# Sixteen experts of a mixture-of-experts stage: order of their matmuls, of the gather and scatter, and of their weight loads

## The chip, the cores and the metric

One core of a Trainium2 chip runs the whole program. The metric is the time of one execution on the device in microseconds, the median of repeated runs.

## The reference

Two transformer blocks run one after the other on 512 tokens of width 1024. Only one stage of the second block is touched, the expert-choice feed-forward: each of 16 experts picks its 64 best tokens, and its answer is added back to them.

```python
def expert_choice_ffn(xn, w_router, w_gate, w_up, w_down):
    cap = CAPACITY_FACTOR * S // N_EXPERTS                     # 64
    aff = softmax(xn @ w_router)                               # 512 x 16
    top_aff, top_idx = lax.top_k(swapaxes(aff, 1, 2), cap)     # per expert
    xg = xn[bidx, top_idx]                                     # gather, 64 x 1024 an expert
    hid = silu(xg @ w_gate) * (xg @ w_up)
    y = (hid @ w_down) * top_aff
    return zeros.at[bidx, top_idx].add(y)                      # scatter
...
h = h + expert_choice_ffn(rmsnorm_2(h, norm_ffn), ...)
ple_gate = sigmoid(rmsnorm_2(h, norm_ple) @ w_ple_gate)
h = h + ple_gate * (p @ w_ple)
return rmsnorm_2(h, norm_final)
```

## The kernel before, in words

Everything ahead of the experts' stage (both mixers, attention, the first block's MLP, the router) is the same in both kernels. A tile framework turns the program text into one instruction list for each engine. Its scheduler goes by program order as a priority and by its own estimate of when data will be there, so a ready instruction can be put ahead of one that the scheduler believes to be waiting; each engine then runs its list strictly in that order.

**Weights.** An expert has three 1024 x 1024 float32 matrices (gate, up, down), loaded as four pieces of 1 MB each: 192 pieces in all. A piece is `wv[:, k:k + 2, :]`, so each of 128 partitions receives two rows of 4 KB that lie 512 KB apart in memory (L806). `load_expert(e + 1)` stands behind expert e in the program; the pieces go into a ring of 15 tiles (`wnext` 12, `wlast` 3), and the first two experts' last pieces into six spare places (`spare`). Twelve pieces are loaded during the output projection ahead of the stage (L1270 to L1275), the others when the stage's pools open. The load instructions are all on SP's queue, in order, and each waits until its ring tile has been read.

**An expert.** 64 tokens make 64 columns of stationary data, so TensorE is used as two halves of 64 columns: the two halves of an output row (512 columns each) go side by side (L1445 for gate and up, L1471 for down). A float32 matmul is two passes in the trace, so gate and up are 64 rows of the trace and down is 32.

1. Gate and up: 64 matmuls into two PSUM banks (`pg`, `pu`).
2. Sigmoid on ScalarE (L1460), two products on VectorE (L1461, L1462).
3. Four transposes on TensorE (L1465), one copy on ScalarE (L1467).
4. Down: 32 matmuls (L1471) that read this copy.
5. `yh`, `yl`: the result times its affinity, split in two parts (ScalarE L1479, VectorE L1480).

**Gather and scatter by pairs.** Experts 2g and 2g+1 share one gather: a one-hot matrix `oh` (VectorE, L1351) picks 128 rows, in eight blocks `rows(k)` of four matmuls (eight rows of the trace, L1360), each block with a ScalarE evacuation into `xg` (L1361). In the text `rows(k + 1)` stands between the gate's matmuls of the even expert; the last pair's gather is taken ahead, behind gate and up of expert 11. Behind the even expert's gate and up come `affinities()` (L1366) and four transposes of `oh` into `gT` (L1457). Behind the odd expert's down come eight scatters: two matmuls (L1483, L1484) and one VectorE addition to `x` (L253) each. The last pair's scatter belongs to the tail, which computes the per-layer gate and the final norm.

**Other work of the stage.** Behind expert 5, `project_p` multiplies `p` by `w_ple` (48 matmuls, L124 to L126). Behind expert 14, `x` is transposed for the tail (L1530). Small pools: `y4` 5 tiles of 4 KB a partition, `m2` 4 tiles of 2 KB. PSUM: `pd` 4 banks, `pscore` 2, `pout` 2.

Software DMAs, issued by GpSimd, occur once, at the start of the second block (13 small loads, L852 to L879).

Of the kernel before, what the change touches and what calls it, by code (L numbers as in the profile page):

```python
# [19 lines left out]
P = 128  # L20
T = 512
# [14 lines left out]
def two_blocks_kernel(ctx: ExitStack, tc: tile.TileContext, A: dict, out: bass.AP, stage: int = 99):  # L36
# [751 lines left out]
    turn = itertools.cycle(["wnext"] * 12 + ["wlast"] * 3)  # L788
# [7 lines left out]
    def load_pieces(e, got):  # L796

        for n in ("w_exp_gate_2", "w_exp_up_2", "w_exp_down_2"):
            wv = A[n][0, e].rearrange("(k p) f -> p k f", p=P)
            for k in range(0, KT, 2):  # L800
                w = spare.pop(0) if e < 2 and len(got) >= 16 + 4 * e else w8()
                if isinstance(w, list):
                    for i in range(2):
                        nc.sync.dma_start(w[i], wv[:, k + i, :])
                else:
                    nc.sync.dma_start(w, wv[:, k:k + 2, :])  # L806
                    w = [w[:, 0, :], w[:, 1, :]]
                got += w
                yield

    spare = []
    started = {}

    def start_expert(e, n):

        if e not in started:
            got = []
            started[e] = got, load_pieces(e, got)  # L820
        for _ in itertools.islice(started[e][1], n):
            pass

    def load_expert(e):
        start_expert(e, 12)
        return started[e][0]


    with ExitStack() as blk:
# [440 lines left out]
        open_ring(late, "wnext", 12, side="right")  # L1270
        start_expert(0, 6)

        def more():
            start_expert(0, 8 - 6)
            start_expert(1, 4)  # L1275
# [32 lines left out]
    with ExitStack() as blk:  # L1308
        pool = blk.enter_context(tc.tile_pool(name="moe", bufs=1, reuse_waits="tile"))
        open_ring(blk, "wlast", 3)  # L1310

        def y4(dt=F32, shape=(D,)):
            return pool.tile([P] + list(shape), dt, name="y4", tag="y4", bufs=5)

        def m2(dt=F32, shape=(T,)):
            return pool.tile([P] + list(shape), dt, name="m2", tag="m2", bufs=4)
# [5 lines left out]
        def pick(ahead=False):  # L1322
            if ahead:
                return m2(shape=(NT, 2, CAP)), y4(shape=(2, KT, CAP))
            return (pool.tile([P, NT, 2, CAP], F32, name="oh", bufs=1),
                    pool.tile([P, 2, KT, CAP], F32, name="xg", bufs=1))

        picked = [pick()]
        w = acts_half(F32, (NT, D), "act_hi")
        spare += [w[:, 0:2, :], w[:, 2:4, :], [y4(), y4()], [y4(), y4()]]  # L1330
# [5 lines left out]
        spare += [w[:, 0:2, :], w[:, 2:4, :]]  # L1336
        ws = load_expert(0)
# [3 lines left out]
        def gather(g):  # L1341

            oh, xg = picked.pop() if picked else pick(ahead=2 * g + 2 == NE)
# [11 lines left out]
            src, sel = (xn[0], oh) if g else (x, scaled)  # L1355

            def rows(k):
                ps = pscore()[:, :P]
                for t in range(NT):
                    PE.matmul(ps, src[:, t, k * P:(k + 1) * P], sel[:, t, :], start=(t == 0), stop=(t == NT - 1))  # L1360
                S.activation(xg[:, :, k, :], ps.rearrange("p (e s) -> p e s", e=2), AF.Copy, scale=gcol[:, k:k + 1])  # L1361
# [9 lines left out]
            return oh, xg, rows, affinities  # L1371

        def load_p():
            pr = w8((NT, 256))
            nc.sync.dma_start(pr, A["p_2"][0, 0].rearrange("(t p) c -> p t c", p=P))
            raw = w8()
            nc.sync.dma_start(raw, A["w_ple_2"][0].rearrange("(k p) c -> p k c", p=P))
            return pr, raw

        def split8(raw):  # L1380
            hi, lo = w8(dt=F32R), w8(dt=F32R)
            S.copy(hi, raw)
            V.tensor_sub(lo, raw, hi.bitcast(F32))
            return hi, lo

        def project_p(pr, raw):
            wh, wl = split8(raw)
            pT = w8((2, 2, T), F32R)
# [41 lines left out]
        oh = xg = None  # L1430
        for e in range(NE):
            if e == NE - 1:
                gfin = row(y4(), A["norm_final_2"])
            if e % 2 == 0 and e + 2 < NE:
                oh, xg, rows, affinities = gather(e // 2)
                rows(0)
            if e == NE - 2:
                oh, xg, _, affinities = ahead
            pg, pu = pd(), pd()
            for i, ps in ((0, pg), (8, pu)):  # L1440
                for k in range(KT):
                    if e % 2 == 0 and e + 2 < NE and i == 0 and k + 1 < KT:
                        rows(k + 1)
                    for half in range(2):
                        PE.matmul(ps[64 * half:64 * half + 64, :], xg[:, e % 2, k, :],  # L1445
                                  ws[i + k][:, 512 * half:512 * half + 512],
                                  start=(k == 0), stop=(k == KT - 1))
            if e == NE - 5:
                ahead = gather(NE // 2 - 1)
                for k in range(KT):  # L1450
                    ahead[2](k)
            if e % 2 == 0:
                affinities()
                yh, yl, gT = y4(F32R), y4(F32R), m2(F32R)
                pt = pout()
                for t in range(NT):
                    PE.transpose(pt[:, t * P:(t + 1) * P], oh[:, t, :], ident)  # L1457
                S.copy(gT, pt)
# [3 lines left out]
            V.tensor_mul(hd, hd, pu)  # L1462
            pt = pout()
            for i in range(4):
                PE.transpose(pt[:, i * P:(i + 1) * P], hd[:, i * P:(i + 1) * P], ident)  # L1465
            hT = m2(shape=(4, P))
            S.copy(hT, pt.rearrange("p (a b) -> p a b", a=4))  # L1467
            py = pscore()
            for k in range(KT):
                for half in range(2):  # L1470
                    PE.matmul(py[64 * half:64 * half + 64, :], hT[:, k % 4, 64 * (k // 4):64 * (k // 4) + 64],  # L1471
                              ws[16 + k][:, 512 * half:512 * half + 512],
                              start=(k == 0), stop=(k == KT - 1))
# [8 lines left out]
            def scatter(t, n, ps):  # L1482
                PE.matmul(ps, gT[:, t * P:(t + 1) * P], yh[:, 512 * n:512 * n + 512], start=True, stop=False)  # L1483
                PE.matmul(ps, gT[:, t * P:(t + 1) * P], yl[:, 512 * n:512 * n + 512], start=False, stop=True)  # L1484
                add_to_x(512 * n)(t, ps)

            last = e == NE - 1 and stage > 7
            if e % 2 and not last:
                for n in range(2):
                    for t in range(NT):  # L1490
                        scatter(t, n, pd())
            if last:
                zh, zl = [[w8((4, T), F32R) for _ in range(2)] for _ in range(2)]
                wg = []
                pss = [pd() for _ in range(NT)]
                todo = [(t, n) for n in range(2) for t in range(NT)]
                for k in range(KT):

                    ps = pout()
                    PE.matmul(ps, yh[:, k * P:(k + 1) * P], gT, start=True, stop=False)  # L1500
                    PE.matmul(ps, yl[:, k * P:(k + 1) * P], gT, start=False, stop=True)
                    zk, hi = xT[k // 4][:, k % 4, :], zh[k // 4][:, k % 4, :]
                    V.tensor_add(zk, zk, ps)
                    S.copy(hi, zk)
                    V.tensor_sub(zl[k // 4][:, k % 4, :], zk, hi.bitcast(F32))
                    if k % 2:
                        wg.append(split_gate(k // 2, wgr[k // 2]))
                        gate_step(pss, k // 2)
                        for _ in range(2):
                            scatter(*todo.pop(0), pscore())  # L1510
            if e == 4:
                praw = load_p()
            if e == 5:
                pp = project_p(*praw)
            if e == 0:
# [4 lines left out]
            if e + 1 < NE:  # L1520
                ws = load_expert(e + 1)
            if e == NE - 2:
                wgr = [load_gate(k) for k in range(0, KT, 2)]

                xT = [w8((4, T)) for _ in range(2)]
                for t in range(NT):
                    for i in range(2):
                        ps = pout().rearrange("p (a b) -> p a b", a=4)
                        for k in range(4):
                            PE.transpose(ps[:, k, :], x[:, t, (4 * i + k) * P:(4 * i + k + 1) * P], ident)  # L1530
                        S.copy(xT[i][:, :, t * P:(t + 1) * P], ps)
# [127 lines left out]
```

## Time and profile before

| | |
|---|---|
| median of 3 runs | 1955.38 us (1954.65 to 1956.43) |
| profiled execution, its own time | 1954.67 us |
| its span, first to last instruction | 1952.9 us |
| TensorE busy | 1878.2 us, 96% of the span |
| VectorE / ScalarE busy | 919.1 us / 718.4 us |
| granted TensorE clock, mean | 0.991 |
| bytes moved | 330.88 MB, 169 GB/s over the span |

The experts' stage runs from about 1383.5 us of the span (first gather) to 1890.9 us (first matmul of the tail). "Busy" of TensorE is modelled at its ends, so the starts of successive matmuls tell more than their durations.

### The profile page before, as it was taken

To read this page: it belongs to the slowest core of one execution; us is meant where nothing else is said; L and a number is where in the kernel's file an instruction comes from. 1 tells how busy PE (TensorE), PEld (TensorE's weight loads), DVE (VectorE), ACT (ScalarE), POOL (GpSimd) and SP (SyncE) were. 2 spreads that over 40 slices of the span, in tenths; PEclk is the share of its full clock that TensorE was granted. 3 is DMA by queue.
4 is the path that set the end of the run, shared out by engine and by line. 5 is a ranking of instruction groups with operands and counts; after the bars stand their busy time and mean duration, and the time that the engine had idled before them with its cause. 6 is when DMAs were issued, how large, how long until landed. Compare 5 with 4: busy or idle time off the path is not lost. (4 is left out here: it accounts for less than half of the span.)

```text
span 1952.9 us, 24468 instructions
## 1 busy us (share of the span) xinstructions
PE 1878.2 (96%) x9723; PEld 1362.9 (70%) x9723; DVE 919.1 (47%) x1659; ACT 718.4 (37%) x1329; POOL 66.9 (3%) x103
## 2 busy tenths in 40 slices
PE   7999999999999999999999999999699999999998
PEld 6777788888888888887787778887344354444346
DVE  5777777465543443436875564453322111111236
ACT  4454774343332322325665554322121121111134
POOL 0000220000000000002000000000000000000000
PEclk9999999999999999999999999999799999999999
DMA  7222226431233333324222222236889999998951
GB/s 206 55 64 72 56 85 189 131 107 55 73 111 98 97 97 97 97 76 112 73 65 57 74 71 70 86 125 247 325 312 402 375 381 401 406 405 334 409 237 44
DMA packets 178052, 330.88 MB, mean 169 GB/s; under 512 B 10766, under 2 KB 90370, under 8 KB 177938
## 3 DMA queue, kind: packets, MB, share of 16 engines
q1 hardware_dynamic: 177522, 328.91, 48.1%
q8 instruction: 77, 1.26, 0.3%
q0 software_dynamic: 416, 0.41, 0.1%
q14 instruction: 37, 0.30, 0.0%
HBM read 327.19 MB, written 2.10 MB: 169 GB/s over the span
## 5 line engine op out<-in xcount | busy, mean ns | idle before, releaser
L104 DVE TENSOR_TENSOR lo<-raw,hi 128x1024 fp32r<-128x1024 f32 x208 | 253.5, 1221 | 324.5 <-ACT hi L103 321.5
L103 ACT CAST hi<-raw 128x1024 fp32r<-128x1024 f32 x208 | 218.0, 1049 | 417.7 <-PE pd L126 230.7
L124 PE MATMUL pd<-hi,act_hi 128*128 128x512 f32 (+2 forms) x584 | 228.2, 391 | 2.0 <-ACT act_hi L206 1.6
L125 PE MATMUL pd<-lo,act_hi 128*128 128x512 f32 (+2 forms) x584 | 226.5, 388 | 0.8 <-DVE lo L104 0.8
L124 PE MATMUL pd<-act_hi,hi 128*128 128x512 f32 (+1 forms) x592 | 224.2, 380 | 0.5 <-ACT act_hi L206 0.5
L126 PE MATMUL pd<-act_hi,lo 128*128 128x512 f32 (+1 forms) x592 | 224.5, 380 | 0.0
L125 PE MATMUL pd<-act_lo,hi 128*128 128x512 f32 (+1 forms) x592 | 224.3, 379 | 0.0
L1445 PE MATMUL pd<-w,xg 128*64 128x512 f32 x896 | 205.3, 598 | 0.0
L126 PE MATMUL pd<-hi,act_lo 128*128 128x512 f32 (+1 forms) x512 | 199.8, 392 | 0.0
L1445 PEld LDWEIGHTS pd<-w,xg 128*64 128x64 f32 x896 | 60.8, 137 | 109.0 <-issue 100.3
L124 PEld LDWEIGHTS pd<-hi,act_hi 128*128 128x128 f32 x584 | 110.3, 189 | 22.7 <-ACT act_hi L206 3.3
L126 PEld LDWEIGHTS pd<-act_hi,lo 128*128 128x128 f32 x592 | 111.5, 188 | 19.5 <-issue 0.2
L125 PEld LDWEIGHTS pd<-act_lo,hi 128*128 128x128 f32 x592 | 111.5, 188 | 19.4 <-DVE act_lo L207 0.5
L124 PEld LDWEIGHTS pd<-act_hi,hi 128*128 128x128 f32 x592 | 111.1, 188 | 19.9 <-ACT act_hi L206 1.0
L125 PEld LDWEIGHTS pd<-lo,act_hi 128*128 128x128 f32 x584 | 110.2, 189 | 20.1 <-DVE lo L104 1.3
L1471 PE MATMUL pscore<-w,m 128*64 128x512 f32 x464 | 107.9, 607 | 6.7 <-ACT m L1467 6.7
L126 PEld LDWEIGHTS pd<-hi,act_lo 128*128 128x128 f32 x512 | 96.7, 189 | 17.9 <-DVE act_lo L207 0.4
L1480 DVE SCALAR_TENSOR_TENSOR y<-pscore,affs,y 64x512 fp32r<-64x512 f32 x32 | 24.0, 750 | 169.2 <-ACT y L1479 168.9
L253 DVE TENSOR_TENSOR x<-x,pd 128x512 f32<-128x512 f32 x111 | 71.9, 684 | 61.9 <-PE pd L126 56.7
L125 PE MATMUL pd<-lo,hh 128*128 128x512 f32 x256 | 99.7, 390 | 0.0
L124 PE MATMUL pd<-hi,hh 128*128 128x512 f32 x256 | 99.7, 389 | 0.0
L126 PE MATMUL pd<-hi,hl 128*128 128x512 f32 x256 | 99.6, 389 | 0.0
(459 smaller groups left out, 2870.9 us busy)
## 6 DMA issues: line engine op xcount, KB each, us to landing
w<-in_w_exp_gate_dram SPq DMA_DIRECT2D x64, 1024.0 KB, 9.1
w<-in_w_exp_up_dram SPq DMA_DIRECT2D x64, 1024.0 KB, 13.8
w<-in_w_exp_down_dram SPq DMA_DIRECT2D x58, 1024.0 KB, 9.0
raw<-in_w_in_dram SPq DMA_DIRECT2D x80, 512.0 KB, 3.6
raw<-in_w_up_dram SPq DMA_DIRECT2D x32, 512.0 KB, 4.2
raw<-in_w_down_dram SPq DMA_DIRECT2D x32, 512.0 KB, 3.6
raw<-in_w_xkv_dram SPq DMA_DIRECT2D x16, 512.0 KB, 4.9
raw<-in_w_out_dram SPq DMA_DIRECT2D x16, 512.0 KB, 3.7
```

What stands on the lines that cost most here:

```text
L103: S.copy(hi[:, :size], raw[:, :size])
L104: V.tensor_sub(lo[:, :size], raw[:, :size], hi[:, :size].bitcast(F32))
L124: PE.matmul(ps, ah, bh, start=first, stop=False)
L125: PE.matmul(ps, ah, bl, start=False, stop=False)
L126: PE.matmul(ps, al, bh, start=False, stop=last)
L253: return lambda t, ps: V.tensor_add(x[:, t, c:c + 512], x[:, t, c:c + 512], ps)
L1445: PE.matmul(ps[64 * half:64 * half + 64, :], xg[:, e % 2, k, :], ws[i + k][:, 512 * half:512 * half + 512], start=(k == 0), stop=(k == KT ...
L1471: PE.matmul(py[64 * half:64 * half + 64, :], hT[:, k % 4, 64 * (k // 4):64 * (k // 4) + 64], ws[16 + k][:, 512 * half:512 * half + 512], s ...
L1480: V.scalar_tensor_tensor(yl[r0:r0 + 64, 512 * half:512 * half + 512], src, sc, h.bitcast(F32), op0=OP.mult, op1=OP.subtract)
```

## The change

The experts run in a pipeline of depth one: gate and up of expert e come before the transposes and down of expert e - 1, so the products and the copy of one expert stand beside matmuls of another. `hidden`, `turned` and `down` are the three parts; `hidden` and `down` take a table `between` that says which closures go behind which step. For odd e, the eight scatters of the pair before stand in `hidden(e)` behind every second step; then `affinities()` and `back()` (the transposes into `gT`); then the eight `rows(k)` of the next pair stand in `down(e - 1)` behind each step (for e = 15 the transposes of `x` instead). Four `rows` blocks share one PSUM bank of `pout`; before, each had a bank of `pscore`.

The loads follow one list in the order of use (`order`), each started when a tile of the ring comes free (`used`). The ring has 17 tiles (12 and 5); six first pieces have places of their own (`homes`), others than before. The host lays the three weight arrays out as one array in which a partition's share of a piece is 8 KB in one run. `y4` shrinks from 5 tiles to 4, `m2` from 4 to 3, `gT` has a tile of its own, and the SBUF area for the descriptors of software DMAs is 2048 bytes a partition.

```diff
-    turn = itertools.cycle(["wnext"] * 12 + ["wlast"] * 3)
+    WNEXT, WLAST = 12, 5
+    turn = itertools.cycle(["wnext"] * WNEXT + ["wlast"] * WLAST)
...
+    order = [(0, m) for m in range(2)]
+    for e in range(1, NE):
+        order += [(e, 0), (e, 1), (e - 1, 2)]
+    order.append((NE - 1, 2))
+    order = [(e, m, q) for e, m in order for q in range(KT // 2)]
...
+        for i, (e, m, q) in itertools.islice(loads, n):
+            wv = A["w_exp"][e, m, q]
...
+                nc.sync.dma_start(w.rearrange("p a b -> p (a b)"), wv.rearrange("p a b -> p (a b)"))
...
+    def used(e, m):
+        room[0] += sum(r for _, r in pieces.pop((e, m))) // 2
+        load(max(0, room[0]))
...
+        homes[12], homes[13] = w[:, 0:2, :], w[:, 2:4, :]
...
+        homes[14], homes[15] = w[:, 0:2, :], w[:, 2:4, :]
+        homes[16 + WLAST], homes[17 + WLAST] = [[y4(), y4()] for _ in range(2)]
...
             def rows(k):
-                ps = pscore()[:, :P]
+                j = k % 4
+                if j == 0:
+                    ps[0] = pout()
...
+        def hidden(e, xg, between):
             pg, pu = pd(), pd()
...
                     for half in range(2):
                         PE.matmul(ps[64 * half:64 * half + 64, :], xg[:, e % 2, k, :],
...
+                    for f in between.get(KT * m + k, ()):
+                        f()
...
+        def down(e, yh, yl, between):
...
+                for f in between.get(k, ()):
+                    f()
+            used(e, 2)
...
+        xg, rows, affinities, back = gather(0)
+        rows(0)
+        hd = hidden(0, xg, each([lambda k=k: rows(k) for k in range(1, KT)], range(KT - 1)))
+        turned(0, hd)
+        for e in range(1, NE):
...
+            todo = [lambda t=t, n=n: scatter(t, n, pd()) for n in range(2) for t in range(NT)] if e % 2 and e > 1 else []
+            hd = hidden(e, xg, each(todo, range(0, 16, 2)))
...
+            if e % 2:
+                affinities()
+                gT = back()
+                yh, yl = y4(F32R), y4(F32R)
+                if e + 1 < NE:
+                    xg, rows, affinities, back = gather((e + 1) // 2)
+                    more = each([lambda k=k, f=rows: f(k) for k in range(KT)], range(KT))
+                else:
+                    wgr = [load_gate(k) for k in range(0, KT, 2)]
+                    xT = [w8((4, T)) for _ in range(2)]
+                    more = each([lambda t=t, i=i: turn_x(t, i) for t in range(NT) for i in range(2)], range(KT))
+            if e == 6:
+                pp = project_p(*praw)
...
+            down(e - 1, yh, yl, more)
...
+            turned(e, hd)
+        gfin = row(y4(), A["norm_final_2"])
+        down(NE - 1, yh, yl, {})
...
-    nc = _bacc.Bacc("TRN2", target_bir_lowering=False, num_devices=1)
+    nc = _bacc.Bacc("TRN2", target_bir_lowering=False, num_devices=1, dynamic_dma_scratch_size=2048)
...
+    w = np.stack([given.pop(f"w_exp_{n}_2")[0] for n in ("gate", "up", "down")], 1)
+    given["w_exp"] = w.reshape(NE, 3, KT // 2, 2, P, D).transpose(0, 1, 2, 4, 3, 5)
```

## Rows read from the trace of the kernel before

**Rows 1.** Busy time by stretch: us, each engine busy (x count), clock, DMA share, GB/s

```profile
1448.80:1508.20 59.40, 58.38 (x293) 26.19 (x292) 11.55 (x21) 9.15 (x21) 0.00 (x0) 1.00 0.92 354
...
1582.50:1649.50 67.00, 61.97 (x306) 28.02 (x305) 10.34 (x19) 10.22 (x23) 0.00 (x0) 0.95 1.01 400
1649.50:1710.70 61.20, 58.19 (x294) 26.12 (x294) 11.62 (x22) 9.15 (x21) 0.00 (x0) 1.00 1.02 401
...
1840.00:1864.00 24.00, 22.91 (x111) 8.17 (x112) 3.05 (x5) 1.18 (x2) 0.00 (x0) 1.00 1.03 409
```

**Rows 2.** Waits of TensorE, 1383 to 1891 us: total us, times, longest

```profile
PE pout L1465 <- DVE m L1462: 11.5, 12, 2.8
PE pscore L1471 <- ACT m L1467: 6.7, 14, 0.9
...
PE pscore L1360 <- ACT y L1361: 1.1, 1, 1.1
...
PEld pd L1445 <- DMA w<-in_w_exp_gate_dram: 2.3, 8, 0.3
```

**Rows 3.** The chain that ended last: start, us, engine, tile, line, count

```profile
1655.10 1.01 PE pd L1445 x4
1656.10 1.09 PE pscore L1360 x8
...
1669.25 7.09 PE pscore L1471 x32
1676.34 13.76 PE pd L1445 x64
...
1692.19 1.94 PE pscore L1471 x8
1694.13 1.09 PE pscore L1360 x8
...
1705.92 0.92 PE pd L1484 x4
...
1742.45 1.54 PE pscore L1360 x12
```

**Rows 4.** Timeline of TensorE around scatters and around `project_p`

```profile
1582.15 0.39 PE L126 MATMUL pd<-w,w 128*128 128x512 f32 x1
1582.47 3.65 PE L1445 MATMUL pd<-w,xg 128*64 128x512 f32 x16
...
1704.72 1.19 PE L1483 MATMUL pd<-y,m 128*128 128x512 f32 x4
...
1710.69 4.51 PE L1445 MATMUL pd<-w,xg 128*64 128x512 f32 x20
...
1834.41 1.21 PE L1483 MATMUL pd<-y,m 128*128 128x512 f32 x4 [0.78 <-ACT y L1479]
...
1839.99 13.95 PE L1445 MATMUL pd<-w,y 128*64 128x512 f32 x64
```

**Rows 5.** Timeline of TensorE, down of expert 6

```profile
1606.27 8.87 PE L1471 MATMUL pscore<-w,m 128*64 128x512 f32 x32 [0.73 <-ACT m L1467]
```

**Rows 6.** Timeline of TensorE, first and last of 74 full-width blocks among half-width ones

```profile
1388.60 1.16 PE L1360 MATMUL pscore<-m,x 128*128 128x128 f32 x8
...
1877.61 1.09 PE L1530 MATMUL pout<-ident,x 128*128 128x128 f32 x8
```

**Rows 7.** DMA queues (packets, MB, share of 16 engines) and SP's longest wait, 1290 to 1900

```profile
q1 hardware_dynamic: 177522, 328.91, 48.1%
...
SPq L806 <- PE pd L1445: 258.3, 111, 19.7
```

**Rows 8.** Groups of ScalarE and VectorE, 1383.5 to 1890.9 us: busy, mean ns | idle before

```profile
L1361 ACT ACTIVATE xg<-pscore,gcol 128x128 f32<-128x128 f32 x56 | 20.6, 368 | 119.4 <-PE pscore L1360 119.4
...
L1519 ACT ACTIVATE act_hi<-x,rs 128x1024 f32<-128x1024 f32 x4 | 4.3, 1136 | 3.9 <-PE pscore L1471 3.9
...
L1351 DVE TENSOR_TENSOR oh<-slots,slot 128x128 f32<-128x128 f32 x28 | 6.3, 287 | 57.2 <-PE pout L1457 53.8 <-PE pscore L1366 3.4
```

More of the change, by code (lines that the diff above doesn't have):

```diff
@@ L794, in w8, with load @@
         return wpools[next(turn)].tile([P] + list(shape), dt, name="w8", tag="w8")
[L796 to L826, printed above, removed]
+    order = [(0, m) for m in range(2)]
[3 more added lines that the diff above has]
+    order = [(e, m, q) for e, m in order for q in range(KT // 2)]
+    pieces = {(e, m): [] for e in range(NE) for m in range(3)}
+    homes = {}
+    loads = iter(enumerate(order))
+    room = [WNEXT + WLAST]
+    def load(n):
+        for i, (e, m, q) in itertools.islice(loads, n):
+            wv = A["w_exp"][e, m, q]
+            if i in homes:
+                w = homes[i]
+            else:
+                w = w8()
+                room[0] -= 1
+            if isinstance(w, list):
+                for j in range(2):
+                    nc.sync.dma_start(w[j], wv[:, j, :])
+            else:
+                nc.sync.dma_start(w.rearrange("p a b -> p (a b)"), wv.rearrange("p a b -> p (a b)"))
+                w = [w[:, 0, :], w[:, 1, :]]
+            pieces[e, m] += [(w[j], i not in homes) for j in range(2)]
+    def used(e, m):
+        room[0] += sum(r for _, r in pieces.pop((e, m))) // 2
+        load(max(0, room[0]))
     with ExitStack() as blk:
@@ L1370, in affinities, with back @@
                         S.copy(affs[64 * half:64 * half + 64, e:e + 1], ps[64 * j:64 * j + 64, e:e + 1])
-            return oh, xg, rows, affinities
+            def back():
+                gT = pool.tile([P, T], F32R, name="gT", bufs=1)
+                pt = pscore()
+                for t in range(NT):
+                    PE.transpose(pt[:, t * P:(t + 1) * P], oh[:, t, :], ident)
+                S.copy(gT, pt)
+                return gT
+            return xg, rows, affinities, back
         def load_p():
@@ L1384, in split8, with project_p @@
             return hi, lo
[L1386 to L1388 removed]
+        def project_p(pr, raw, hi, lo, pT):
+            wh, wl = split8(raw, hi, lo)
             for t in range(NT):
@@ L1429, in two_blocks_kernel @@
         xn = []
[L1430 to L1438, printed above, removed]
+        hT = {}
+        def hidden(e, xg, between):
             pg, pu = pd(), pd()
-            for i, ps in ((0, pg), (8, pu)):
+            for m, ps in enumerate((pg, pu)):
                 for k in range(KT):
-                    if e % 2 == 0 and e + 2 < NE and i == 0 and k + 1 < KT:
-                        rows(k + 1)
+                    w = pieces[e, m][k][0]
                     for half in range(2):
                         PE.matmul(ps[64 * half:64 * half + 64, :], xg[:, e % 2, k, :],
[L1446 to L1458, printed above, removed]
+                                  w[:, 512 * half:512 * half + 512], start=(k == 0), stop=(k == KT - 1))
+                    for f in between.get(KT * m + k, ()):
+                        f()
+            for m in range(2):
+                used(e, m)
             hd = m2()
@@ L1481, in two_blocks_kernel @@
                                        op0=OP.mult, op1=OP.subtract)
[L1482 to L1510, printed above, removed]
@@ L1511, in two_blocks_kernel, with scatter, each @@
-            if e == 4:
-                praw = load_p()
+        def scatter(t, n, ps):
+            PE.matmul(ps, gT[:, t * P:(t + 1) * P], yh[:, 512 * n:512 * n + 512], start=True, stop=False)
+            PE.matmul(ps, gT[:, t * P:(t + 1) * P], yl[:, 512 * n:512 * n + 512], start=False, stop=True)
+            add_to_x(512 * n)(t, ps)
+        def each(fs, places):
+            b = {}
+            for f, i in zip(fs, places):
+                b.setdefault(i, []).append(f)
+            return b
@@ L1519, in two_blocks_kernel @@
                     S.activation(xn[0][:, t, :], x[:, t, :], AF.Copy, scale=rx[t][:, 0:1])
[L1520 to L1531, printed above, removed]
+            more = {}
@@ new lines, in two_blocks_kernel @@
+            if e == 6:
+                pp = project_p(*praw)
+                room[0] += 5
+            down(e - 1, yh, yl, more)
+            if e == 5:
+                praw = load_p()
+            turned(e, hd)
+        gfin = row(y4(), A["norm_final_2"])
+        down(NE - 1, yh, yl, {})
+        zh, zl = [[w8((4, T), F32R) for _ in range(2)] for _ in range(2)]
+        wg = []
+        pss = [pd() for _ in range(NT)]
+        todo = [(t, n) for n in range(2) for t in range(NT)]
+        for k in range(KT):
+            ps = pout()
+            PE.matmul(ps, yh[:, k * P:(k + 1) * P], gT, start=True, stop=False)
+            PE.matmul(ps, yl[:, k * P:(k + 1) * P], gT, start=False, stop=True)
+            zk, hi = xT[k // 4][:, k % 4, :], zh[k // 4][:, k % 4, :]
+            V.tensor_add(zk, zk, ps)
+            S.copy(hi, zk)
+            V.tensor_sub(zl[k // 4][:, k % 4, :], zk, hi.bitcast(F32))
+            if k % 2:
+                wg.append(split_gate(k // 2, wgr[k // 2]))
+                gate_step(pss, k // 2)
+                for _ in range(2):
+                    scatter(*todo.pop(0), pscore())
```

63 lines of the change are left out of this document (34 added, 29 removed).

## The prediction

> **What bounds the kernel now.** I read the page first (TensorE 96% busy), then busy time by stretch, the waits, the chain and the timeline of the experts' stage. The page's 96% hides the question, since the change touches only the stage from 1383.5 to 1890.9 us. There two things are nearly full at once. Pair 4 (experts 8 and 9) takes 61.2 us with the DMA engines at a share of 1.02, and the stretch from 1840 to 1864 us moves 409 GB/s at 1.03 [rows 1]. Yet TensorE almost never waits for weights: 2.3 us in eight waits for gate's, none above 0.3 us [rows 2]. SP is the one that waits: 258.3 us in 111 waits for gate and up matmuls to free a ring tile [rows 7]. So TensorE sets the pace, and the transfers keep up with little to spare. TensorE's own losses are waits on the way from gate and up to down: 11.5 us in 12 waits for the last product, 6.7 us in 14 for the copy [rows 2].
>
> A second loss is less plain. Half-width matmuls run at 13.76 / 64 = 0.215 us each, so four need 0.86; between two gather blocks they take 1.01, which is 0.15 more. Twelve gather matmuls take 1.54 and eight take 1.09, so one costs 0.1125 and a block of eight should take 0.90; it takes 1.09, 0.19 more [rows 3]. One full-width block put among half-width matmuls thus costs 0.34 us beyond its work. I count 74 such blocks over the stage [rows 6], about 25 us. The new text weaves far more of them.
>
> The Trainium skill says that a change of tiling mode, not of the tile alone, drains TensorE (TensorEngine Tiling (Array Packing), Key Properties). The rows above agree and put 0.34 us on it; the page gives no duration, so the sum by the rule is the sum by the rows, and without the rule's drain weaving would be free and the stage 18 us shorter than I reckon below.
>
> **The change, part by part.** Figures are TensorE time in the profiled execution, whose stage lasts 507.4 us.
>
> *Pipelining by one* removes the waits for the last product (11.5) and the copy (6.7) [rows 2], except the last expert's copy (0.7), behind which nothing is left to run: 17.5. The products and the copy of expert e then stand beside down of expert e - 1, which is 7.09 us [rows 3]; VectorE and ScalarE are busy 11.6 and 9.2 of pair 4's 61.2 us [rows 1], so the cover is ample, and without it they would cost what they cost now. Late next would be the ring tiles, treated below. The longest of these waits, 2.8 us in pair 3, is followed by down at 8.87 instead of 7.09 [rows 3, 5], in a stretch with a mean granted clock of 0.95 [rows 1], partly at the lower of the two levels: 1.8 more go with it.
>
> *Scatters in the next odd expert's gate and up.* Today pair 6's eight scatters run alone, from 1834.41 to 1839.99 after a wait of 0.78: 6.4 us [rows 4]. A matmul of this kind takes 0.92 / 4 = 0.23 [rows 3], sixteen take 3.7; so 2.7 go. In pairs 0 to 5 they are mixed with gathers: from 1704.72 to 1710.69 there are 16 scatter and 16 gather matmuls, 3.7 + 1.8 = 5.5 of 5.97 us [rows 4]; 0.5 each, 3 in all. Woven, each addition has the time of two steps, so nothing waits for a bank. The gather taken ahead waits 1.1 once [rows 2]. Removed here: 6.8. Removed in all: 17.5 + 1.8 + 6.8 = 26.1.
>
> *What weaving adds.* As written, full-width blocks among half-width matmuls number 56 scatters (7 pairs of 8), 7 gathers in expert 0, 8 of affinities with `back`, 56 gathers (the transposes stand right behind the last of each group), 8 transposes of `x`, 8 transposes behind even experts, and 1 for `project_p`: 144, against 74 [rows 6]. The 88 that are not scatters cost 0.34 each; 14 more than now make 4.8. A scatter between half-width matmuls is not in the trace. The nearest row is the way from the full-width L126 to L1445: 1582.15 to 1582.47, 0.32 against 0.23 [rows 4], so 0.09 on leaving a block of long matmuls, to which I add the 0.15 on the half-width side: 0.24. From below it is that 0.15 alone, from above 0.6, if both weight loads show. I take 0.24, since a matmul of 0.23 us can cover the second weight load as a gather of 0.11 cannot: 56 x 0.24 = 13.4.
>
> *New waits.* The next pair's one-hots (four at 0.22 to 0.29, 0.9 to 1.15 us [rows 8]) can start only when `back` has read the old ones, and the first `rows` waits for them with a step of 1.0 us ahead: 0 to 0.9, I take 0.4, seven times, 2.8. Everything behind it on TensorE waits too. `xn` (4 x 1.14 on ScalarE [rows 8]) now waits for half of up of expert 1, because its place holds those weights: 0 to 4, I take 1, once. Four `rows` blocks share a bank, so a block waits for the evacuation before it, 0.37 [rows 8]; a down step of 1.0 us lies between, so 0, and 0.5 a block at worst where two come together. `affinities` and `back` hold both `pscore` banks when down wants one: 0 to two evacuations (0.7), I take 0.15 a pair, 1.2. Sum 5.
>
> *What the scheduler joins.* Its order is not the text's: the gather block at 1694.13 stands in down of expert 9 [rows 3], though the text puts it at expert 10. Blocks that it joins save their 0.24 to 0.34. Of 112 woven blocks I take an eighth, 14, as joined, 4 back; the ends are none and half of them, 16.
>
> *Longer packets and the ring.* The 48.1% of 16 engines in 1952.9 us are 15,029 us for 177,522 packets and 328.91 MB [rows 7]; 409 GB/s means 160 ns for a 4 KB packet [rows 1]. Taking a packet as a fixed part plus its bytes, both hold with a fixed part of 22 ns; it is less if waiting makes up some of the sum. So 1 MB takes 2.56 us now and 2.38 to 2.56 with 8 KB; I take the middle, 2.47. A pair's 24 pieces need 59.3 us, and a pair of the new order about 60 on TensorE. Over the stage, the 180 pieces that remain and 1.6 MB for `project_p` need 449 us, or 465 at 4 KB, of 507. With 17 tiles as lead the transfers stay hidden, and I cost them at 0. If that cover goes, a pair takes 61.5, 1.5 more, eight times.
>
> *Smaller pools, scratch, layout.* The software DMAs lie outside the stage, are 13, and none of the waits of the stage names them: 0, a few us at most. `y4` and `m2` hold what is live at once (a pair's `yh` and `yl` twice; one `hd`, two `hT`): 0, at most an evacuation's 0.4 a pair. The tail keeps its order.
>
> The sum: -26.1 + 4.8 + 13.4 + 5 - 4 = -6.9. 1954.67 - 6.9 = 1947.8 for that execution; the median of the runs lies 0.7 above it, so 1948.5.
>
> **The rivals.** A difference below 0.2% (3.9 us) can't be told from none.
> 1. *Given back in full.* The mechanism holds, but nothing is joined and the new waits double: -26.1 + 18.2 + 10 = 2.1, 1957.5; the case spans 1951.5 to 1959.3. For it: both sums are large and nearly equal. Against it: each of the waits is bounded by an idle engine.
> 2. *Slower: a woven scatter shows its weight loads.* The place is the 56 scatters in gate and up. Each 0.1 above 0.24 costs 5.6, so from 0.43 on the kernel is slower by 0.2%, and at 0.6 it takes 1968.7. For it: a gather block's first matmuls show such a delay. Against it: the 0.32 behind L126 [rows 4].
> 3. *Better.* The scheduler joins half of the woven blocks (16 instead of 4) and the new waits vanish (5): 1931.5; the case spans 1931 to 1941. For it: scatters and gathers that stand together cost almost no switching, 5.97 for 5.5 of work [rows 4]. Against it: the new text puts them at different matrices.
> 4. *The loads become the bound.* 8 KB packets gain nothing, the lead is used up, and pairs stop at 61.5: 12 more, 1960.5, less what the lead saves. Against it: pair 1 took 59.4 with a share of only 0.92 [rows 1].
>
> **How the numbers follow.** The forecast case (1941 to 1951.5) has 48%, rival 3 20%, rivals 1 and 4 together 18%, rival 2 14%. Faster is 48 + 20 = 68%, same 18%, slower 14%. The likeliest time is 1948.5. A range from 1934 to 1960 leaves out about a third of rival 3 below and nearly all of rival 2 above, two in ten.
>
> **What would show it.** The waits of transposes for the products and of down for the copy should be gone but for one. Gate and up with eight scatters should last 13.76 + 3.7 + 1.9 = 19.4 us. Whole pairs should be even, near 60 us. SP should still wait for TensorE; a TensorE wait for weights above 1 us would prove the transfers' part wrong. Packets of 8 KB should take 300 to 320 ns. I am wrong if the stage's length goes with the DMA share and not with the number of blocks, or if anything before 1383 us moves.

## The result, and the profile after

The changed kernel takes 1970.59 us (median of 4 runs, 1970.44 to 1971.90) against 1955.02 for the kernel before in the same session: 1.0083 times as long, 95% interval 1.0070 to 1.0095. That is 0.8% slower, where 0.35% faster was predicted, and it lies above the predicted range. The profiled execution took 1970.57 us, its span 1968.8.

Nearly all of it lies in the experts' stage. From the first gather to the first matmul of the tail it lasted 507.3 us before and 524.7 after (1382.59 to 1907.27), 17.4 more; it starts 0.9 us earlier, and what follows is 0.5 shorter. Below, "stage" is this stretch, a "block" is a run of full-width matmuls (gathers, scatters, transposes) between half-width ones, and "the slow clock" is the lower of TensorE's two clock levels.

Busy time by stretch, after; the columns are those of [rows 1]:

```profile
1443.50:1503.00 59.50, 59.22 (x280) 23.09 (x278) 12.16 (x20) 8.59 (x20) 0.00 (x0) 1.00 0.95 379
1580.00:1640.00 60.00, 54.60 (x234) 26.16 (x230) 13.87 (x22) 12.75 (x25) 0.00 (x0) 0.94 0.90 367
1640.00:1700.00 60.00, 59.72 (x282) 23.50 (x280) 12.15 (x20) 8.87 (x20) 0.00 (x0) 1.00 0.99 403
1880.00:1907.00 27.00, 22.70 (x108) 9.47 (x104) 2.25 (x4) 7.01 (x13) 0.00 (x0) 0.94 0.04 16
```

TensorE is busy nearly throughout, except in the stretches from 1580 and from 1880 us; in both the mean granted clock is 0.94. The DMA share of these rows stays at 0.99 or below, where it reached 1.03 before [rows 1]; from 1850 to 1880 us it is 1.01. SP still waits for TensorE to read the ring's tiles, 387.5 us in 162 waits from 1290 to 1900 us (total us, times, longest):

```profile
SPq L822 <- PE pd L1450: 225.1, 110, 11.1
SPq L822 <- PE pscore L1475: 162.4, 52, 11.4
```

The transfers are no nearer to being the bound. TensorE's waits in the stage, after, in the same columns; [rows 2] answers to it:

```profile
PE pd L124 <- ACT w L206: 4.6, 1, 4.6
PE pout L1465 <- DVE m L1459: 3.9, 5, 0.8
PE pscore L1381 <- ACT affs L1374: 3.8, 5, 0.8
PE pout L1504 <- ACT w L1505: 2.9, 1, 2.9
PE pout L1362 <- ACT xg L1364: 1.6, 3, 0.5
PE pd L1491 <- DVE y L1486: 1.1, 4, 0.3
PE pout L1362 <- DVE m L1347: 1.0, 1, 1.0
PE pscore L1475 <- ACT affs L1374: 0.8, 3, 0.3
...
PE pscore L1475 <- ACT m L1467: 0.7, 1, 0.7
```

The 11.5 us of waits for the last product are 3.9 now (L1465), the 6.7 for the copy are 0.7 (L1475 behind L1467), and none is for weights. But three others have come, in four rows: for `project_p`'s copy (L124), for the bank in which the affinities stand (L1381 and L1475, behind L1374), for the copies of the turned `x` (L1504). Over all rows of this view, TensorE waited 24.7 us before and 21.2 after: the two waits that the change was to remove fell by 13.6 us, and all others together rose by 10.1.

Taken together the waits thus fell by 3.5 us, and they can't be what added 17.4. What was added shows on TensorE's timeline in gate and up of expert 7 (start, duration, line, count):

```profile
1624.40 1.94 PE L1450 MATMUL pd<-w,xg 128*64 128x512 f32 x8
1626.27 0.50 PE L1490 MATMUL pd<-y,gT 128*128 128x512 f32 x1
1626.61 0.40 PE L1491 MATMUL pd<-y,gT 128*128 128x512 f32 x1
1626.93 1.94 PE L1450 MATMUL pd<-w,xg 128*64 128x512 f32 x8
```

From 1624.40 to 1626.93 are 2.53 us. Eight half-width matmuls (0.215 each [rows 3]) and two of a scatter (0.23) need 2.18. A woven scatter thus costs 0.35 us beyond its work, as much as a gather block does [rows 3], and not the 0.24 of the prediction: 0.15 is lost on the half-width side, 0.11 between the scatter's two matmuls (1626.27 to 1626.61 is 0.34), 0.09 on the way out (1626.61 to 1626.93 is 0.32). Counted on the trace, the stage has 127 blocks, against 75 before (the prediction's 74 and the gathers that open the stage): 52 more, by 0.35 are 18.2 us.

The transfers did what was said of them. The 8 KB packets took a median of 313 ns, and the queue moved the same bytes in fewer packets [rows 7]:

```profile
q1 hardware_dynamic: 153202, 328.91, 47.0%
```

### The profile page after: what moved, and what is told of

Same layout as the page of the kernel before. It is cut to its first block, busy times and chain, and to the rows that moved or that the text cites. A ratio compares the mean times of both kernels' runs of the same rounds, so it can differ in the third digit from the quotient of the medians.

```text
span 1968.8 us, 24441 instructions
## 1 busy us (share of the span) xinstructions
PE 1898.0 (96%) x9723; PEld 1357.6 (69%) x9723; DVE 922.0 (47%) x1659; ACT 718.6 (36%) x1329; POOL 67.1 (3%) x103
## 4 chain that ended last, share of the span: by engine, by line
PE 81%; DVE 8%; ACT 5%; issue 2%; DMA 2%; POOL 1%; SPq 0%; POOLq 0%; ACTq 0%; DVEq 0%
PE pd L125 16%; PE pd L124 16%; PE pd L126 16%; PE pd L1450 12%; PE pscore L1475 6%; PE pout L1362 4%; DVE lo L104 2%; ACT hi L103 1%; PE pd L1490 1%; PE pout L1126 1%; PE pout L204 1%; PE pd L1491 1%; POOL rs L188 1%; PE pscore L400 1%; PE pout L1023 1%
## 5 line engine op out<-in xcount | busy, mean ns | idle before, releaser
L124 PE MATMUL pd<-hi,act_hi 128*128 128x512 f32 (+2 forms) x584 | 227.8, 390 | 2.0 <-ACT act_hi L206 1.6
L1450 PE MATMUL pd<-w,xg 128*64 128x512 f32 x976 | 228.5, 601 | 0.0
L124 PE MATMUL pd<-act_hi,hi 128*128 128x512 f32 (+1 forms) x592 | 224.1, 380 | 0.5 <-ACT act_hi L206 0.5
L126 PE MATMUL pd<-act_hi,lo 128*128 128x512 f32 (+1 forms) x592 | 224.5, 379 | 0.0
L126 PE MATMUL pd<-hi,act_lo 128*128 128x512 f32 (+1 forms) x512 | 199.9, 391 | 0.3 <-DVE act_lo L207 0.3
L1450 PEld LDWEIGHTS pd<-w,xg 128*64 128x64 f32 x976 | 65.1, 137 | 121.4 <-issue 119.7
L1475 PE MATMUL pscore<-w,m 128*64 128x512 f32 x512 | 124.8, 604 | 1.5 <-ACT affs L1374 0.8
L124 PEld LDWEIGHTS pd<-hi,act_hi 128*128 128x128 f32 x584 | 110.2, 189 | 22.7 <-ACT act_hi L206 3.3
L126 PEld LDWEIGHTS pd<-act_hi,lo 128*128 128x128 f32 x592 | 111.5, 188 | 19.4 <-issue 0.2
L124 PEld LDWEIGHTS pd<-act_hi,hi 128*128 128x128 f32 x592 | 111.1, 188 | 19.9 <-ACT act_hi L206 1.0
L126 PEld LDWEIGHTS pd<-hi,act_lo 128*128 128x128 f32 x512 | 96.6, 189 | 18.1 <-DVE act_lo L207 0.7
L124 PE MATMUL pd<-hi,hh 128*128 128x512 f32 x256 | 99.7, 389 | 0.0
L126 PE MATMUL pd<-hi,hl 128*128 128x512 f32 x256 | 99.6, 389 | 0.0
```

The lines of the kernel that those rows point to most:

```text
L124: PE.matmul(ps, ah, bh, start=first, stop=False)
L126: PE.matmul(ps, al, bh, start=False, stop=last)
L1475: PE.matmul(py[64 * half:64 * half + 64, :], h[:, k % 4, 64 * (k // 4):64 * (k // 4) + 64], w[:, 512 * half:512 * half + 512], start=(k == ...
```

## The experiments

The theory: TensorE sets the pace before and after; each insertion of full-width work costs about 0.35 us, 52 more of them cost more than the removed waits gave (18.2 against 13.6), and new waits, most of them behind instructions in ScalarE's queue, came on top. Rivals: the loads (ring, layout) are what became slower; the waits alone did it; the pipelining itself does not pay.

| kernel | blocks | stage, us | median, us | against before (95%) |
|---|---|---|---|---|
| before | 75 | 507.3 | 1955.02 | |
| after | 127 | 524.7 | 1970.59 | 1.0083 (1.0070 to 1.0095) |
| e1_scatter_pairs | 105 | 515.8 | 1962.48 | 1.0041 (1.0026 to 1.0056) |
| e2_gather_fours | 107 | 517.3 | 1964.78 | 1.0052 (1.0037 to 1.0067) |
| e3_split_early | 127 | 525.3 | 1971.53 | 1.0090 (1.0074 to 1.0107) |
| e4_packets_4k | 127 | 524.6 | 1971.01 | 1.0085 (1.0070 to 1.0100) |
| e5_three_waits | 122 | 510.8 | 1957.68 | 1.0017 (1.0008 to 1.0026) |
| e6_one_block | 22 | 479.5 | 1926.26 | 0.9856 (0.9840 to 0.9873) |
| e7_not_pipelined | 127 | 524.3 | 1965.87 | 1.0060 (1.0045 to 1.0075) |
| e8_interleaved | 22 | 467.3 | 1913.35 | 0.9789 (0.9773 to 0.9806) |
| e9_block_4k | 22 | 480.3 | 1926.54 | 0.9861 (0.9846 to 0.9875) |
| e10_block_not_pipelined | 29 | 500.1 | 1947.74 | 0.9964 (0.9951 to 0.9977) |
| e11_interleaved_4k | 22 | 473.4 | 1922.04 | 0.9834 (0.9817 to 0.9850) |

Blocks and stage are taken from each kernel's profiled execution, as for the two kernels above; each ratio is to runs of the kernel before in the same session. Line numbers shift in the experiments; the tiles' names tell which line is meant.

**e1: scatters in pairs.**

```diff
-            hd = hidden(e, xg, each(todo, range(0, 16, 2)))
+            hd = hidden(e, xg, each(todo, (1, 1, 5, 5, 9, 9, 13, 13)))
```

> Two scatters stand together at every fourth weight step of an odd expert's gate and up, instead of one at every second: 28 insertions in place of 56. Theory (TensorE pays about 0.35 us for each full-width block that stands among half-width matmuls): 28 x 0.35 = 9.8 us less, 1960.8 us. Rival (the new waits alone made the change slower, insertions are nearly free): within 2 us of 1970.6. Rival (weight loads or the ring set the pace): within 2 us of 1970.6.

It gained 8.1 us. The scheduler had joined some scatters before, so 22 blocks went and not 28; the stage is 8.9 shorter, 0.40 a block. In that are a slow clock that is gone at the turned `x` (0.9 in all) and, the other way, 1.6 us more of waits (2.2 new ones for additions to `x`). Both rivals fall.

**e2: gathers by four.**

```diff
-                    more = each([lambda k=k, f=rows: f(k) for k in range(KT)], range(KT))
+                    more = each([lambda h=h, f=rows[1]: f(h) for h in range(2)], (2, 6))
...
+            def rows4(h):
+                ps[0] = pout()
+                for j in range(4):
+                    for t in range(NT):
+                        PE.matmul(ps[0][:, j * P:(j + 1) * P], src[:, t, (4 * h + j) * P:(4 * h + j + 1) * P],
```

> The eight gather blocks of the next pair go into down in two groups of four (behind weight steps 2 and 6) instead of one at each step; each group has a bank of its own and is evacuated when it is complete. 56 insertions in down become 14. Theory: 42 x 0.34 = 14.3 us less, and up to 1.6 us of waits for the bank's evacuation less: 1955 to 1957 us. Rival (insertions are nearly free): within 2 us of 1970.6. Rival (loads set the pace): within 2 us of 1970.6.

Only 5.8 us. The size failed for a reason that the trace shows: of 42 blocks no more than 20 went, because the scheduler set the turned transposes of the expert, which had stood beside a gather block, apart (17 such blocks in place of 7). They then wait for the bank:

```profile
PE pout L1476 <- ACT xg L1375: 3.9, 3, 1.3
```

The stage is 7.4 shorter, 0.37 a block, in spite of 1.7 us more of waits.

**e3: split early, by the text alone.** The two instructions of `split8` are written ahead of `hidden(6)`.

```diff
+            if e == 6:
+                wp = split8(*praw[1:4])
             hd = hidden(e, xg, each(todo, range(0, 16, 2)))
...
-                pp = project_p(*praw)
+                pp = project_p(praw[0], *wp, praw[4])
```

> The split of w_ple is written ahead of expert 6's gate and up instead of inside project_p behind them. Theory: project_p's wait of 4.64 us goes, and with it the slow clock that follows, 64 matmuls of which about 15 us ran partly at the lower level, some 3 us: 1963 us. Rival (the wait comes back at another instruction, since down of expert 5 still ends just before): 1968 to 1971 us.

No gain: 1971.53. The timeline shows why (the bracket is the idle time and what ended it):

```profile
1593.53 0.68 ACT L1484 ACTIVATE y<-pscore,affs 64x512 fp32r<-64x512 f32 x1 [0.81 <-DVE y L1485]
...
1594.23 1.90 ACT L1394 CAST w<-w 128x2048 fp32r<-128x2048 f32 x1
...
1596.15 0.65 ACT L206 CAST w<-pout 128x256 fp32r<-128x256 f32 x2
...
1596.58 0.80 PE L124 MATMUL pd<-w,w 128*128 128x512 f32 x1 [4.64 <-ACT w L206]
```

The text was moved, the instruction was not: the scheduler still put the split (L1394) behind the evacuations of down(5), at its old place. ScalarE's list is run in order, and the copy of the transposes (L206) starts when the split ends, so TensorE waits the same 4.64 us.

**e4: packets of 4 KB**, in the changed kernel.

```diff
-                nc.sync.dma_start(w.rearrange("p a b -> p (a b)"), wv.rearrange("p a b -> p (a b)"))
+                nc.sync.dma_start(w, wv)
...
-    given["w_exp"] = w.reshape(NE, 3, KT // 2, 2, P, D).transpose(0, 1, 2, 4, 3, 5)
+    given["w_exp"] = w.reshape(NE, 3, KT // 2, 2, P, D)
```

> Nothing is changed but the layout of the experts' weights in memory: packets of 4 KB as before, with every compute engine's order as in the changed kernel. Theory (TensorE sets the pace, loads are hidden): within 2 us of 1970.6. Rival (loads set the pace): 180 pieces at 2.56 instead of 2.47 us, 1980 us or more. Rival (the longer packets themselves cost time, by contention): faster than 1967 us.

1971.01, with every compute engine's order the same. The layout costs and gives nothing here, and both rivals fall.

**e5: three orders held.** Issue order is forced, with no wait for the instruction's end.

```diff
+                for i in split8(*praw[1:4]):
+                    queued.enter_context(tc.issue_after(i))
             hd = hidden(e, xg, each(todo, range(0, 16, 2)))
...
+                    for t in range(NT):
+                        for i in range(2):
+                            last = turn_x(t, i)
+                    for i in last:
+                        queued.enter_context(tc.issue_after(i.ins))
...
-            turned(e, hd)
+            with tc.issue_after(end):
+                turned(e, hd)
```

> The changed kernel with three orders held: the split of w_ple stands on its engines ahead of expert 6's sigmoid, products and the evacuation of down(5); the eight transposes of x stand in one block ahead of down(14), their copies ahead of its evacuation; an expert's turned transposes stand behind down of the expert before. 122 blocks instead of 127. Theory: the wait in project_p (4.64) with its slow clock (3) goes, the wait at the transposes of x (2.95) with its slow clock (2) goes, their copies pace the block (1.2 more), the five waits for products (3.9) go, five blocks fewer (1.7): 17 us less, 1953.5 us. Rival (the waits move to the next instruction in line, and only the number of blocks counts): 1968 to 1970 us.

It gained 12.9 of the 17, and the stage is 13.9 shorter. Its waits, as far as they are of these three:

```profile
PE pd L124 <- ACT w L206: 2.7, 1, 2.7
...
PE pout L1462 <- DVE m L1456: 0.8, 1, 0.8
...
PE pout L1502 <- ACT w L1503: 0.4, 2, 0.2
```

Products fell from 3.9 to 0.8, the turned `x` from 2.9 to 0.4. `project_p` fell only from 4.6 to 2.7: the 1.9 us of its split are out of the way now, but the copy of its transposes (L206) still stands behind both evacuations. The rival was right on that one. The waits are thus a second part of the loss, beside the blocks: with 7.5 of their 11.4 us gone and 122 blocks left, the kernel is still 0.2% slower than the one before (0.1 to 0.3).

**e6: one block a pair.** The full-width work of a pair stands in this order behind down of the even expert, with TensorE's order held; the split of `w_ple` is written early as in e3, and `project_p` stands one expert later:

```diff
+            hd = hidden(e, xg, {})
...
+            down(e - 1, yh, yl, {})
...
+            for t, n in todo[:4]:
+                scatter(t, n, pd())
+            gT = back()
...
+            for t, n in todo[4:]:
+                scatter(t, n, pd())
...
+                rows[1](0)
+                turned(e, hd)
+                rows[1](1)
+                affinities()
```

> Pipelined by one as in the changed kernel, but nothing is woven: behind down of the even expert, all full-width work of a pair stands in one block (scatters of the pair before, back transposes, gathers of the next pair in two groups of four, affinities, turned transposes), and TensorE's order in the stage is held as written. 22 blocks instead of 127; gT has a second buffer. Theory (each block 0.335 us, waits as listed): 105 blocks are 35 us less, the waits for split, transposes of x, products and affinities (15) go, the block's additions and evacuations show some 13 us: 1933 us, 1925 to 1945. Rival (the loads become the bound as TensorE gets faster): 1945 to 1955 us with TensorE waits for weights. Rival (uncovered additions and evacuations take back what the blocks save): 1955 us or more.

1926.26, 44 us under the changed kernel and 28 under the one before. The stage is 45.2 us shorter; TensorE's waits are 14.6 instead of 19.4 without those that both have, so 40.4 us go with 105 blocks, 0.38 each (a changed clock is in that too, and no run holds TensorE's order without taking blocks away). Its waits lie where the block has no cover, at the evacuated gathers, the additions to `x` and `project_p`:

```profile
PE pout L1376 <- ACT xg L1380: 5.6, 7, 0.9
PE pd L1506 <- DVE x L258: 5.4, 7, 0.8
PE pout L209 <- DVE w L212: 2.4, 1, 2.4
```

**e7: the weaving without the pipelining.**

```diff
+    order = [(e, m) for e in range(NE) for m in range(3)]
...
+            turned(e, hd)
...
+            down(e, yh, yl, more)
```

> The changed kernel with its weaving (as many blocks, 127), but down of an expert directly behind its own turned transposes, weights in the order gate, up, down; scatters stand in the next even expert's gate and up, gathers in down of the odd expert; two pieces fewer are loaded ahead at the start. Theory (the pipelining as such gives what the waits of before held): 4.6 us of waits for products and copies become 18 again, 1984 us, 1980 to 1988. Rival (the pipelining as such is worth nothing or costs): 1972 us or less.

The theory said 1984; it took 1965.87, 4.7 less than the changed kernel. This is a miss, and it corrects the theory. The waits for products and copy did come back:

```profile
PE pout L1461 <- DVE m L1455: 11.1, 14, 0.8
PE pd L124 <- ACT w L206: 4.6, 1, 4.6
PE pscore L1471 <- ACT m L1463: 4.3, 7, 0.7
```

But the theory had forgotten the waits that the changed kernel's own order brings. Those for the affinities' bank, the gathers' evacuations, the turned `x` and the scatters' input (3.8 + 0.8, 1.6, 2.9 and 1.1) fell to 0.5, and the slow clock at the turned `x` went with them. In the order that the changed kernel has, the pipelining bought 10.8 us of waits with nearly as many others. What makes e7 4.7 us faster is not fully accounted for: its profiled execution took 1968.30, the longest of its four, and in its stage stand eight scatter matmuls (1.8 us) that the other kernels have in the tail, so that its 524.3 can't be set beside theirs. Whether the pipelining can pay was left to e10.

**e8: the block in another order.**

```diff
+            turned(e, hd)
             gT = back()
...
+            for t, n in todo[:2]:
+                scatter(t, n, pd())
+            if e + 1 < NE:
+                rows[1](0)
+            for t, n in todo[2:5]:
+                scatter(t, n, pd())
...
                 rows[1](1)
+            for t, n in todo[5:]:
+                scatter(t, n, pd())
```

> The kernel with one block a pair, its block in another order: turned and back transposes first, then two scatters, four gather blocks, three scatters, four gather blocks, three scatters, affinities, so that each addition and each evacuation has other matmuls beside it. 22 blocks as before. Theory: its waits for the evacuated gathers (5.6) and for the additions to x (5.4) go, 11 us less than 1926.3: 1915 us, 1913 to 1920. Rival (the waits move to other instructions of the block, since VectorE's and ScalarE's work in it is nearly as long as TensorE's): 1922 us or more. Rival (the loads become the bound): 1920 to 1926 with TensorE waits for weights.

1913.35: 12.9 less than e6, and 2.1% under the kernel before, the fastest of the study. Those two waits are gone but for 0.6, the one in `project_p` fell to 0.9, and the slow clock there is gone (the mean granted clock from 1604 to 1612 us is 0.57 in e6; in e8 it is 1.00 from 1390 to 1850). For the first time TensorE waits for weights:

```profile
PE pscore L1490 <- DMA w<-in_w_exp_dram: 3.8, 5, 1.6
PE pd L1465 <- DMA w<-in_w_exp_dram: 1.3, 3, 0.6
```

**e9 and e11: 4 KB packets in e6 and in e8**, by the edit of e4.

> The kernel with one block a pair (1926.3), with packets of 4 KB in place of 8 KB, every engine's order the same. Theory (the transfers stay hidden even with a stage of 480 us): within 2 us of 1926.3. Rival (the layout was needed once TensorE is faster): 1930 us or more, with TensorE waits for weights.

> The fastest kernel so far (one block a pair, interleaved, 1913.3), with packets of 4 KB in place of 8 KB and every engine's order the same. In it TensorE waits 5.1 us for weights, and the DMA engines move 420 GB/s at a share of 1.01 from 1625 to 1805 us, where 4 KB packets gave 409 at 1.03. Theory (here the loads have just become the bound, so the layout now counts): 2.6% less over the 260 us in which the share is above 1, so up to 7 us of additional waits for weights, 1916 to 1921 us. Rival (the layout is worth nothing here either): within 2 us of 1913.3.

e9 took 1926.54, no difference. e11 took 1922.04, 8.7 more than e8, a little over what was expected; the stage is 6.1 longer, of which 4.5 are waits for weights (9.6 against 5.1). Its waits and a stretch, and the same stretch of e8:

```profile
PE pscore L1490 <- DMA w<-in_w_exp_dram: 5.0, 8, 0.7
PE pd L1465 <- DMA w<-in_w_exp_dram: 4.6, 7, 0.9
```

```profile
1685.00:1745.00 60.00, 60.00 (x318) 27.62 (x316) 11.64 (x21) 8.37 (x21) 0.00 (x0) 1.00 1.03 409
1745.00:1805.00 60.00, 55.64 (x290) 24.98 (x288) 11.56 (x20) 8.37 (x21) 0.00 (x0) 1.00 1.03 409
```

```profile
1685.00:1745.00 60.00, 60.00 (x318) 27.63 (x316) 12.29 (x21) 8.36 (x21) 0.00 (x0) 1.00 1.01 419
1745.00:1805.00 60.00, 58.38 (x310) 26.96 (x308) 11.60 (x20) 8.35 (x21) 0.00 (x0) 1.00 1.01 420
```

The layout gives 420 GB/s in place of 409, and that counts only where the loads bound the stage.

**e10: e6 without the pipelining.**

```diff
+            if e + 1 < NE:
+                turned(e, hd)
+                down(e, yh, yl, {})
...
-            down(e - 1, yh, yl, {})
```

> The kernel with one block a pair (1926.3) without the pipelining: down of an expert directly behind its own turned transposes; 29 blocks instead of 22. The last expert alone keeps its block ahead of down. w_ple is loaded one expert later, and two pieces fewer are loaded ahead. Theory (the pipelining as such is worth its waits where nothing else is put in the way): 15 waits of about 1.2 us and 7 blocks of 0.35 come back, 1946 us, 1940 to 1950. Rival (the pipelining is worth nothing here either, as with the weaving): 1930 us or less.

1947.74, 21.5 more than e6; the stage is 20.6 longer, of which 17.9 are waits and 7 blocks at 0.35 are 2.5. The waits that came back are those of the kernel before:

```profile
PE pout L1476 <- DVE m L1470: 11.1, 14, 0.8
PE pscore L1486 <- ACT m L1478: 10.3, 15, 0.9
```

With nothing woven, the pipelining is worth about the 17.5 us of waits that the prediction took it for. Beside e7 that says that the mechanism is sound, and that the order around it took its gain.

## Why the prediction was wrong

The sum was -6.9; the stage gave +17.4. The difference of 24.3 us is in four terms. Two steps failed: the price of a woven scatter, by which the blocks cost more than the removed waits gave, and, larger, the new waits, which were taken as small because the engines behind them are idle on average.

- **The price of a woven scatter** failed, the step that took 0.24 "since a matmul of 0.23 us can cover the second weight load as a gather of 0.11 cannot". It is 0.35. The one row behind it, 0.32 after L126 [rows 4], shows only the way out of a block; the missing 0.11 is lost between the scatter's two matmuls. The count was right (144 less 14 is 130; there are 127). Blocks cost 18.2 where 14.2 was put: 4.0. That is the place of rival 2, short of its point of 0.43, so it alone doesn't decide.
- **The waits** were put at -17.5, -1.1 and +5, so -13.6; they fell by 3.5, an error of 10.1, the largest. The removal was 3.9 short, in five waits. In four of them (experts 4, 10, 12 and 14) the scheduler set the turned transposes of an even expert right behind its gate and up, ahead of down, which is the order that the change undoes; the fifth is expert 0's, which has no down before it. And the new waits were looked for in the wrong place. Those for one-hots and `xn` do not show. Those that do are behind in-order queues: 4.6 for the evacuations of down(5) and the split in `project_p`, whose position the prediction never priced; 2.9 at the turned `x`, costed only as eight insertions; and 4.6 for the affinities' bank, put at 1.2. The sentence "each of the waits is bounded by an idle engine" failed: idle on average, ScalarE still had the evacuation of down ahead in its queue, which waits for TensorE.
- **The slow clock** of pair 3 was to go (-1.8). It went from down of expert 6 and came back in two places, behind the two long waits, about 2.9 us in `project_p` and 0.9 at the turned `x`: +2.0, an error of 3.8.
- **The losses among the scatters** (2.7 + 3.0) were to go and for the most part did not. By the starts of matmuls, blocks with scatters lost 3.7 us before beyond their work, their waits and 0.35 each; they lose 3.4 after. What was counted as loss in pair 6 was in part such an insertion, and in part 1.4 us of waits that stand above. What the account leaves over, with all that no other term names, is +0.7 where -5.7 was put: 6.4.

The turned transposes of expert 4, right behind its own gate and up, on the timeline after:

```profile
1505.52 13.95 PE L1450 MATMUL pd<-w,xg 128*64 128x512 f32 x64
1520.26 0.66 PE L1465 MATMUL pout<-ident,m 128*128 128x128 f32 x4 [0.79 <-DVE m L1459]
```

The turned `x` is the plainest of the queue waits. On the same timeline:

```profile
1879.18 0.60 PE L1504 MATMUL pout<-ident,x 128*128 128x128 f32 x4
...
1883.20 7.04 PE L1475 MATMUL pscore<-w,m 128*64 128x512 f32 x32
...
1891.83 0.68 ACT L1485 ACTIVATE y<-pscore,affs 64x512 fp32r<-64x512 f32 x1 [0.81 <-DVE y L1486]
1892.54 1.07 ACT L1505 COPY w<-pout 128x512 f32<-128x512 f32 x2
...
1893.18 4.72 PE L1504 MATMUL pout<-ident,x 128*128 128x128 f32 x24 [2.95 <-ACT w L1505]
```

Two groups of transposes ran early, the last at 1879. Their copies (L1505) stand behind the evacuation of down(14) (L1485), both banks stay full, and the six other groups could not be woven into down at all. e5, in which they stand ahead, leaves 0.4 of the 2.95.

What held: TensorE sets the pace and the loads stay hidden (e4, e9; the point from which they don't is e8); the 8 KB packets (313 ns, within 300 to 320); the 0.34 of a gather block; the copy wait of the last expert (0.7); the worth of the pipelining, once nothing stands in its way (e10); and of the signs of being wrong, the stage's length does not go with the DMA share. Odd gate and up with eight scatters was to last 19.4 us; that of expert 9 lasts 21.6 (1671.40 to 1692.99), of which 13.76 + 3.7 are work; eight insertions at 0.35 are 2.8, and most of the rest goes to one scatter whose two matmuls the scheduler set apart, a ninth block. Pools, ring of 17 and scratch were not tried apart; no wait of either trace names them. The mistake in the price was to make an exception for the longer matmuls. The Trainium skill says that a change of tiling mode drains TensorE (TensorEngine Tiling (Array Packing), Key Properties). The 0.35 us agrees with that, for scatters as for gathers; no run here separates such a drain from weight loads that show.

## What to carry to other kernels

Count the changes between matmul shapes before weaving small work into a long stream: here each insertion cost 0.35 us, and the same work in one block a pair, in a held order in which evacuations have cover, took 57 us off the changed kernel (blocks, waits and slow clock together). Pipelining pays only as far as the order of the in-order queues allows: look at what stands ahead of a copy in its engine's queue, not at how idle that engine is. And moving text need not move an instruction under a scheduler (e3); read the order that came out, and hold it where it matters.

## What the runs showed of the hardware that was not expected

- The price of an insertion hardly depends on what is inserted: from the last half-width start before the block to the first after it, one, two or five scatter matmuls of 0.23 us took 0.72 to 0.74 us more than their own time, and a gather block of eight at 0.11 took 0.72 more. Of that, 0.42 is the half-width pair that is still running (two matmuls that start 0.01 us apart, a pair every 0.43); 0.05 more is lost in the first pair behind the block. That makes 0.35.
- After 4.64 us without a matmul, `project_p`'s matmuls started every 0.43 us instead of 0.23, at the lower of the two clock levels (1.2 instead of 2.4 GHz), until 1603.3, 5.5 us later. The granted clock, in the columns of [rows 1], is 0.50 there and 1.00 behind it:

```profile
1598.00:1603.00 5.00, 5.00 (x14) 3.58 (x15) 3.25 (x5) 0.75 (x2) 0.00 (x0) 0.50 0.98 385
1604.00:1609.00 5.00, 5.00 (x24) 4.12 (x23) 0.00 (x0) 2.35 (x4) 0.00 (x0) 1.00 0.59 211
```

- One core drew 420 GB/s with 8 KB packets and 409 with 4 KB packets in the old layout, 2.7% apart (e8 and e11), and that came to 8.7 us of the median, 6.1 of them in the stage, once TensorE had caught up with the loads.
